# Gaps of 32 bytes between the tiles that the matmuls read, in a four-layer decoder trunk

## Chip, core and metric

The kernel runs on one core of one Trainium2 chip. The metric is the device time of one execution in microseconds (us); the time before is the median of two runs. The profile is one further look at one execution, taken by the hardware profiler.

## The reference

A trunk of two layers on 512 tokens of width 1024, everything in float32. Each layer is a half-step SwiGLU feed-forward block, an attention block and a second half-step SwiGLU block, all with RMS norm ahead of them:

```python
def swiglu(h, w_gate_up, w_down):
    gate, up = jnp.split(h @ w_gate_up, 2, axis=-1)      # 1024 -> 2 x 2816
    return (jax.nn.silu(gate) * up) @ w_down             # 2816 -> 1024

for i in range(DEPTH):                                   # DEPTH = 2
    x = x + 0.5 * swiglu(rms_norm(x, ...), ffn_w_gate_up[i, 0], ffn_w_down[i, 0])
    h = rms_norm(x, norm_gains[i, 1])
    x = x + (stick_breaking_attention(h, ...) if i % 2 == 0 else sliding_window_attention(h, ...))
    x = x + 0.5 * swiglu(rms_norm(x, ...), ffn_w_gate_up[i, 1], ffn_w_down[i, 1])
```

The first attention block weights each key by a sigmoid times the product of what the later keys left over; the second is a windowed softmax with 16 query heads on 2 key heads. Both end with an output projection of 1024 by 1024.

## The kernel before

**Layout.** The residual stream stays on the chip as eight tiles `x0` to `x7` of 128 channels by 512 tokens. Every large product puts weights into the tensor engine as the stationary operand (128 by 128) and streams 512 tokens past them.

**Three passes.** To keep float32 accuracy, each operand is split into a high part and the rest: `norm_tile` (L244) makes `xh` and `xl` of each tile of x, `_part` (L173) makes `whi` and `wlo` of each piece of weights, `swiglu` (L303) makes `hh` and `hl` of each tile of the activations. `terms` (L127) then issues three matmuls for each 128 rows of the contraction: (`whi`, `xh`), (`whi`, `xl`), (`wlo`, `xh`), always in this order. In the profile the group `gu<-xh,whi` is the first of these for the gate and up products, `dn<-hl,whi` the second for the down product. All have the line L75, that of the helper through which the tensor engine's instructions keep the order of the program.

**Stages.** The string "0s12w3" names six stages: feed-forward 0, stick-breaking attention s, feed-forward 1 and 2, window attention w, feed-forward 3. A feed-forward stage (`ffn`, L317) makes 44 products `gu` of 8 x 3 matmuls (22 gates, 22 ups) and then 8 products `dn` of 22 x 3. So the four of them hold 4 x 44 x 24 = 4224 matmuls for gate and up (24 of them in the first stage write to a bank named `gus`) and 4 x 8 x 66 = 2112 for down. `project_out` (L546) makes the 8 x 24 matmuls `op` at the end of an attention stage; `q` and `k` are 8 x 24 each; `tok` are products with 256 columns in which the weights are streamed.

**Weights.** They come as a stream of units of 128 x 1024 or 128 x 896 numbers. A unit is loaded by DMA (`_load`), then copied to `whi` by ScalarE (L181) and subtracted to `wlo` by VectorE (L186, or GpSimd L184). Three units are held at a time, in three buffers of the tag `whi` and three of `wlo`; when the last matmul of a unit has been issued, `release` (L188) opens the next one. Twice, near the end of an attention stage, `advance` (L166) puts one more unit into tiles that the stage no longer needs (`qsw`/`ksw` in stage s, `qw` in stage w).

**Addresses.** A tile is a run of bytes at one address in all partitions. The tiles lie in the order of their allocation, each rounded up to 32 bytes. In the program before, these are the addresses modulo 128 bytes:

| tiles | remainder |
|---|---|
| x, raw, whi, wlo, acc, xh, xl (all of 2048 or 4096 bytes, one behind the other) | 96 |
| everything of a feed-forward stage: hh, hl (behind three small tiles of 32 bytes each) | 64 |
| stage s: qs, ks, kl, v, wt, the attention outputs o..h and o..l, and the spare weights qsw, ksw | 64 |
| stage w: outputs oh, ol | 96 |
| stage w: spare weights qw | 0 |

Slices of a tile that the matmuls read begin at multiples of 512 bytes from its start, so they have their tile's remainder. So a `gu` matmul streams from remainder 96 and its weights lie at 96; a `dn` matmul streams from 64 and its weights lie at 96.

Of the kernel before, what the change touches and what calls it, by code (L numbers as in the profile page):

```python
# [7 lines left out]
F32 = mybir.dt.float32  # L8
F32R = mybir.dt.float32r
# [6 lines left out]
P = 128  # L16
T = 512
TB = T // P
D = 1024
KD = D // P  # L20
# [4 lines left out]
HD = 64  # L25
# [13 lines left out]
NROT = ROT // 2  # L39
# 500000 ** (-arange(0, 16, 2) / 16) in float32  # L40
INV_FREQ = [
# [23 lines left out]
class _Ordered:  # L65
    """an engine whose instructions stay in the order of the program"""

# [19 lines left out]
class _Filler:  # L87
    """tensor-engine work that fills the waits of an attention step: a generator that yields its cost,
    or None when nothing is ready"""

# [17 lines left out]
class _Trunk:  # L108
    def __init__(self, tc, pools, psum, aps):
        self.tc, self.nc = tc, _Engines(tc)  # L110
        self.const, self.work = pools
        self.psum = psum
        self.aps = aps
        self.units = []
        self.raw, self.ready = [], []
        self.taken = self.spent = 0
        self.roped = False
        self.extra = -1

# [1 line left out]
    def mm(self, out, lhs, rhs, start, stop):  # L121
# [5 lines left out]
    def terms(self, out, pairs, first=True, last=True, release=()):  # L127
        """out = sum of w * x over pairs ((w_hi, w_lo), (x_hi, x_lo)): three float32r passes each;
        release: the terms that are the last of a unit of the weight stream, or 1: the last"""
        n = len(pairs)  # L130
        cost = 3 * max(out.shape[-1], 256) / 2400.0
        for i, ((wh, wl), (xh, xl)) in enumerate(pairs):
            self.mm(out, wh, xh, start=(first and i == 0), stop=False)
            self.mm(out, wh, xl, start=False, stop=False)
            self.mm(out, wl, xh, start=False, stop=(last and i == n - 1))
            if i in ((n - 1,) if release == 1 else release):
                self.release(1)
            yield cost
# [7 lines left out]

# [1 line left out]
    def queue(self, ap, pool=False):  # L148
# [11 lines left out]
    def _open(self, n):  # L160
        size = self.units[n][1]
        hi = self.work.tile([P, size], F32R, tag="whi", name=f"whi{n}", bufs=UNITS)
        lo = self.work.tile([P, size], F32R, tag="wlo", name=f"wlo{n}", bufs=UNITS)
        self.ready.append((hi, lo))

    def advance(self, hi, lo):  # L166
        """one more unit of the weight stream ahead, in tiles that the stage has free"""
        n = self.extra = len(self.ready)
        self.ready.append((hi, lo))
        self._part(n)  # L170
        self._load()
# [25 lines left out]
    def weights(self, a):  # L197
        """the next unit of the stream as [row, a, column] high and low parts"""
        hi, lo = self.ready[self.taken]
        self.taken += 1  # L200
        h3, l3 = (t.rearrange("p (a b) -> p a b", a=a) for t in (hi, lo))
        return [(h3[:, i, :], l3[:, i, :]) for i in range(a)]

# [1 line left out]
    def setup(self, which):  # L205
# [36 lines left out]

# [1 line left out]
    def norm_tile(self, k, which):  # L244
        nc, w = self.nc, self.work
        if k == 0:
            self.xh, self.xl = [], []
            self.acc = w.tile([P, T], F32, tag="acc", name="acc", bufs=1)
        g = self.gain[:, which * KD + k : which * KD + k + 1]
        hi = w.tile([P, T], F32R, tag=f"xh{k}", name=f"xh{k}", bufs=1)  # L250
        lo = w.tile([P, T], F32R, tag=f"xl{k}", name=f"xl{k}", bufs=1)
        nc.scalar.activation(hi, self.x[k], AF.Copy, scale=g)
        nc.vector.scalar_tensor_tensor(lo, self.x[k], g, hi, ALU.mult, ALU.subtract)  # L253
        self.xh.append(hi)
        self.xl.append(lo)
        if k == 0:
            nc.scalar.activation(self.acc, self.x[k], AF.Square)
        else:
            sq = w.tile([P, T], F32, tag="rbc", name="sq", bufs=1)
            nc.scalar.activation(sq, self.x[k], AF.Square)  # L260
            (nc.gpsimd if k < POOL_SQUARES else nc.vector).tensor_add(self.acc, self.acc, sq)  # L261
# [39 lines left out]

# [1 line left out]
    def swiglu(self, fp, f, gu):  # L303
        nc = self.nc
        g = fp.tile([P, T], F32, tag="g", name="g", bufs=2)
        u = fp.tile([P, T], F32, tag="u", name="u", bufs=2)
        nc.vector.tensor_mul(g, gu[0], self.rbc)  # L307
        nc.scalar.activation(g, g, AF.Silu)
        nc.vector.tensor_mul(u, gu[1], self.rbc)  # L309
        nc.vector.tensor_mul(u, g, u)  # L310
        hi = fp.tile([P, T], F32R, name=f"hh{f}")
        lo = fp.tile([P, T], F32R, name=f"hl{f}")
        nc.scalar.copy(hi, u)
        nc.vector.tensor_sub(lo, u, hi)
        return hi, lo
# [52 lines left out]

# [1 line left out]
    def stack(self, out, src):  # L370
        """a pair of heads (rows) to one [high | low] or [low | high] column of rows per head"""
        nc = self.nc
        for h in range(2):
            own, other = slice(h * HD, (h + 1) * HD), slice(HD - h * HD, 2 * HD - h * HD)
            nc.scalar.copy(out[own, h, :], src[own, :])
            nc.vector.tensor_sub(out[other, h, :], src[own, :], out[own, h, :])  # L376

    def project_pair(self, p, out, start=False):
        """q^T and k^T of a pair of heads, as exact high and low parts"""
        nc, ap = self.nc, self.ap  # L380
# [30 lines left out]
    def token_columns(self, evacuate, rows=None):  # L411
        """a chunk of 256 columns of an input projection, tokens on partitions"""
        w = self.weights(KD // 2) + self.weights(KD // 2)
        for b in range(TB):
            sl = slice(b * P, (b + 1) * P)
            ps = self.bank("tok")[:, : 4 * HD]
            yield from self.terms(ps, [((h[:, sl], l[:, sl]), w[k]) for k, (h, l) in enumerate(zip(self.xh, self.xl))], release=(KD // 2 - 1, KD - 1) if b == TB - 1 else ())
            if rows and b == 0:
                rows()
            evacuate(b, ps)  # L420

    def project_values(self, out):
        """v of four heads: [token, block, head, high | low]"""
        nc = self.nc
# [11 lines left out]
    def stick_scores(self, i, qk, out):  # L436
        """exclusive products of the kept lengths times beta, for one pair of heads and query block i"""
        nc, ap = self.nc, self.ap
# [25 lines left out]
    def stick_turn(self, i, beta, wt):  # L464
        """weights of query block i to keys on partitions, high and low parts"""
        nc = self.nc
# [47 lines left out]
    def fold(self, o, h, ps):  # L514
        """the products with the high and the low part of v are on rows of their own: add them"""
        t = self.ap.tile([HD, T], F32, tag="tmp", name="fold", bufs=2)
# [10 lines left out]
    def project_early(self, parts, opened):  # L527
        """the first terms of the first output tiles, as far as parts are there"""
        self.settled, self.spare = len(parts), None
# [79 lines left out]

# [1 line left out]
    def rope_tables(self):  # L611
        """cos | cos and -sin | sin of every token's angles: [token, block, 16]"""
        self.roped = True
# [58 lines left out]

# [1 line left out]
    def rope(self, x, heads, engine):  # L674
        """x: [token, block, heads * HD], rotated in place"""
        nc, ap = self.nc, self.ap
# [11 lines left out]
    def head_factor(self, sq, heads, extra):  # L688
        """r * rsqrt(mean of squares of r * raw + eps) * extra, one per token, block, head"""
        nc, ap = self.nc, self.ap  # L690
# [57 lines left out]
    def window_queries(self, c, out):  # L748
        """four heads of q with head dims on partitions (two heads a tile), and their score factors"""
        nc, ap = self.nc, self.ap  # L750
# [20 lines left out]
    def window_scores(self, c, b, qt, y, out):  # L771
        """the softmax of four heads and one block of queries"""
        nc, ap = self.nc, self.ap
# [161 lines left out]

# [1 line left out]
    def store(self, n):  # L937
# [92 lines left out]
```

## Time and profile before

| | us |
|---|---|
| median of 2 runs (lowest, highest) | 1928.41 (1927.27, 1929.55) |
| profiled execution, first to last instruction | 1925.5 |
| TensorE busy | 1895.7 |
| VectorE busy | 970.5 |
| ScalarE busy | 695.1 |
| GpSimd busy | 172.0 |

The profiled execution's own span is 1925.5 us; between it and the median lie 2.9 us, which stand for what is around the span. A matmul's own duration in a row (some 390 ns) is longer than its share of the engine, since matmuls overlap; the pace is read from the distance of their starts.

### The profile page before, as it was taken

The page shows a single profiled execution, that of the slowest core. Times are in us where ns is not written, and L with a number is a line of the kernel's source. Part 1 is how long each engine was busy: PE and PEld are TensorE (multiplying, and loading weights), DVE is VectorE, ACT ScalarE, POOL GpSimd, SP SyncE. Part 2 cuts the span into 40 slices and gives each one's busy share as a digit, 9 for nine tenths or more (in the row PEclk, how much of TensorE's full clock was granted, in tenths as well). Part 3 has the DMA queues.
Part 4 walks back from the last instruction along what each step waited for, and adds up shares of the span by engine and source line. Part 5 has one row for each costly group of instructions (what it writes and reads, how often), then busy time and mean ns, then how long its engine had stood idle before and what let it go on. Part 6 is the DMA issues. An engine that isn't in the chain of part 4 may idle for free.

```text
span 1925.5 us, 22581 instructions
## 1 busy us (share of the span) xinstructions
PE 1895.7 (98%) x8994; PEld 1565.6 (81%) x8994; DVE 970.5 (50%) x1535; ACT 695.1 (36%) x1071; POOL 172.0 (9%) x131
## 2 busy tenths in 40 slices
PE   9999999999999999999999999999998999999999
PEld 7888888877887888888888888888887788888887
DVE  6444433378887644443235444423588664444321
ACT  5333222266675323332223333222357542223211
POOL 1000000233321000000000000000142210000000
PEclk9999999999999999999999999999989999999999
DMA  5233333321112333223333222333221122332331
GB/s 167 98 97 99 96 91 92 103 69 56 49 62 66 99 97 97 92 97 94 97 96 99 92 98 96 93 93 100 81 67 34 29 92 98 99 99 90 103 109 60
DMA packets 49930, 170.52 MB, mean 89 GB/s; under 512 B 5921, under 2 KB 6177, under 8 KB 49825
## 3 DMA queue, kind: packets, MB, share of 16 engines
q1 hardware_dynamic: 49824, 169.07, 27.9%
q8 instruction: 71, 1.16, 0.2%
q14 instruction: 35, 0.28, 0.0%
HBM read 166.96 MB, written 2.10 MB: 88 GB/s over the span
## 4 chain that ended last, share of the span: by engine, by line
PE 84%; DVE 8%; issue 4%; ACT 3%; POOL 1%; DMA 0%; SPq 0%; ACTq 0%; DVEq 0%; POOLq 0%
PE gu L75 49%; PE dn L75 23%; PE op L75 4%; PE tok L75 3%; DVE keep L459 2%; DVE beta L460 1%; PE pv L75 1%; DVE qs L376 1%; DVE wt L482 1%; ACT keep L453 1%; PE sc L75 1%; PE z L75 0%; PE ptr L75 0%; DVE e L793 0%; PE q L75 0%
## 5 line engine op out<-in xcount | busy, mean ns | idle before, releaser
L181 ACT CAST whi<-raw 128x1024 fp32r<-128x1024 f32 (+2 forms) x323 | 330.0, 1022 | 964.8 <-issue 361.6
L75 PE MATMUL gu<-xh,whi 128*128 128x512 f32 x1400 | 545.5, 390 | 1.4 <-ACT whi L181 1.4
L75 PE MATMUL gu<-xh,wlo 128*128 128x512 f32 x1400 | 545.0, 389 | 0.7 <-DVE wlo L186 0.7
L75 PE MATMUL gu<-xl,whi 128*128 128x512 f32 x1400 | 544.8, 389 | 0.5 <-DVE xl L253 0.5
L186 DVE TENSOR_TENSOR wlo<-raw,whi 128x1024 fp32r<-128x1024 f32 (+2 forms) x293 | 349.4, 1193 | 248.2 <-ACT whi L181 245.6
L75 PEld LDWEIGHTS gu<-xh,wlo 128*128 128x128 f32 x1400 | 262.8, 188 | 56.5 <-DVE wlo L186 1.8
L75 PEld LDWEIGHTS gu<-xh,whi 128*128 128x128 f32 x1400 | 262.9, 188 | 56.2 <-ACT whi L181 1.9
L75 PEld LDWEIGHTS gu<-xl,whi 128*128 128x128 f32 x1400 | 262.9, 188 | 55.3 <-DVE xl L253 0.9
L75 PE MATMUL dn<-hh,wlo 128*128 128x512 f32 x704 | 280.9, 399 | 0.0
L75 PE MATMUL dn<-hl,whi 128*128 128x512 f32 x704 | 277.4, 394 | 0.0
L75 PE MATMUL dn<-hh,whi 128*128 128x512 f32 x704 | 276.0, 392 | 0.0
L309 DVE TENSOR_TENSOR u<-gu,rbc 128x512 f32<-128x512 f32 x87 | 60.1, 691 | 274.7 <-PE gu L75 274.7
L75 PEld LDWEIGHTS dn<-hl,whi 128*128 128x128 f32 x704 | 132.1, 188 | 34.3
L75 PEld LDWEIGHTS dn<-hh,whi 128*128 128x128 f32 x704 | 132.2, 188 | 31.5
L75 PEld LDWEIGHTS dn<-hh,wlo 128*128 128x128 f32 x704 | 132.2, 188 | 30.5
L307 DVE TENSOR_TENSOR g<-gu,rbc 128x512 f32<-128x512 f32 x88 | 60.8, 691 | 176.5 <-PE gu L75 176.4
L261 POOL TENSOR_TENSOR acc<-acc,sq 128x512 f32<-128x512 f32 x30 | 46.4, 1547 | 1116.1 <-ACT sq L260 1116.1
L184 POOL TENSOR_TENSOR wlo<-raw,whi 128x512 fp32r<-128x512 f32 x60 | 87.5, 1483 | 164.9 <-ACT whi L181 164.9
L75 PE MATMUL tok<-whi,xh 128*128 128x256 f32 x288 | 86.4, 300 | 0.0
L75 PE MATMUL tok<-whi,xl 128*128 128x256 f32 x288 | 82.4, 286 | 0.1
L75 PE MATMUL tok<-wlo,xh 128*128 128x256 f32 x288 | 82.3, 286 | 0.1
L300 DVE SCALAR_TENSOR_TENSOR x<-dn,x 128x512 f32<-128x512 f32 x32 | 22.1, 691 | 116.5 <-PE dn L75 116.5
(310 smaller groups left out, 1957.4 us busy)
## 6 DMA issues: line engine op xcount, KB each, us to landing
raw<-in_gu_dram SPq DMA_DIRECT2D x173, 512.0 KB, 3.4
raw<-in_dn_dram SPq DMA_DIRECT2D x64, 448.0 KB, 3.3
raw<-in_dn_dram SPq DMA_DIRECT2D x32, 512.0 KB, 3.5
raw<-in_sbqk_dram SPq DMA_DIRECT2D x16, 512.0 KB, 3.4
raw<-in_swin_dram SPq DMA_DIRECT2D x10, 512.0 KB, 3.5
raw<-in_sbv_dram SPq DMA_DIRECT2D x8, 512.0 KB, 3.3
raw<-in_sbo_dram SPq DMA_DIRECT2D x8, 512.0 KB, 3.5
raw<-in_swo_dram SPq DMA_DIRECT2D x8, 512.0 KB, 3.3
```

Source lines behind the costliest of these rows:

```text
L75: return self._tc.keep_in_program_order(method(*args, **kwargs))
L181: nc.scalar.copy(hi[:, s], raw[:, s])
L184: nc.gpsimd.tensor_sub(lo[:, t], raw[:, t], hi[:, t])
L186: nc.vector.tensor_sub(lo[:, s], raw[:, s], hi[:, s])
L261: (nc.gpsimd if k < POOL_SQUARES else nc.vector).tensor_add(self.acc, self.acc, sq)
L300: self.nc.vector.scalar_tensor_tensor(self.x[n], ps, factor, self.x[n], ALU.mult, ALU.add)
L307: nc.vector.tensor_mul(g, gu[0], self.rbc)
L309: nc.vector.tensor_mul(u, gu[1], self.rbc)
L376: nc.vector.tensor_sub(out[other, h, :], src[own, :], out[own, h, :])
L453: nc.scalar.activation(keep[:, :, :n], z[:, :, :n], AF.Sigmoid, scale=-0.125)
L459: nc.vector.tensor_tensor_scan(rev, rev, rev, 1.0, ALU.mult, ALU.bypass)
L460: nc.vector.tensor_mul(beta[:, :, : n - 1], beta[:, :, : n - 1], keep[:, :, 1:n])
```

## The change

`shift` allocates a tile that nothing uses, of 32 bytes per partition (64 in one place), so that what is allocated behind it begins that much later. There is one ahead of each of the three `whi` and `wlo` buffers, ahead of each of the eight `xh` and `xl`, and ahead of each of the 22 `hh` and `hl` of a feed-forward stage. To have gaps between them, the three buffers of `whi` become three tags with one buffer each, taken by the number of the unit modulo 3; the same for `wlo`. No instruction is added or removed.

```diff
+        self.gaps = 0
+        self.normed = False
+
+    def shift(self, pool, size):
+        self.gaps += 1
+        pool.tile([P, size // 4], F32, name=f"gap{self.gaps}")
...
     def _open(self, n):
         size = self.units[n][1]
-        hi = self.work.tile([P, size], F32R, tag="whi", name=f"whi{n}", bufs=UNITS)
-        lo = self.work.tile([P, size], F32R, tag="wlo", name=f"wlo{n}", bufs=UNITS)
+        if n < UNITS:
+            self.shift(self.work, 32)
+        hi = self.work.tile([P, size], F32R, tag=f"whi{n % UNITS}", name=f"whi{n}", bufs=1)
+        if n < UNITS:
+            self.shift(self.work, 32)
+        lo = self.work.tile([P, size], F32R, tag=f"wlo{n % UNITS}", name=f"wlo{n}", bufs=1)
...
     def norm_tile(self, k, which):
...
+        first = not self.normed
+        self.normed = k == KD - 1 or self.normed
+        if first:
+            self.shift(w, 32)
         hi = w.tile([P, T], F32R, tag=f"xh{k}", name=f"xh{k}", bufs=1)
+        if first:
+            self.shift(w, 32)
         lo = w.tile([P, T], F32R, tag=f"xl{k}", name=f"xl{k}", bufs=1)
...
     def swiglu(self, fp, f, gu):
...
+        self.shift(fp, 64 if f == NF // 2 else 32)
         hi = fp.tile([P, T], F32R, name=f"hh{f}")
+        self.shift(fp, 32)
         lo = fp.tile([P, T], F32R, name=f"hl{f}")
```

Added up in the order of allocation, the remainders modulo 128 become:

| tiles | remainder |
|---|---|
| whi, wlo of buffer 0; 1; 2 | 0, 32; 64, 96; 0, 32 |
| xh, xl of even k; of odd k | 64, 96; 0, 32 |
| hh, hl for f up to 10: even f; odd f | 32, 64; 96, 0 |
| hh, hl for f from 11: even f; odd f | 64, 96; 0, 32 |
| stage s, all of its tiles | 0 |
| stage w: oh, ol; qw | 32; 64 |

## Prediction

> **What bounds the kernel now.** First the page: busy shares, granted clock, and the chain that ended last.
>
> ```profile
> span 1925.5 us, 22581 instructions
> PE 1895.7 (98%) x8994; PEld 1565.6 (81%) x8994; DVE 970.5 (50%) x1535; ACT 695.1 (36%) x1071; POOL 172.0 (9%) x131
> PEclk9999999999999999999999999999989999999999
> PE 84%; DVE 8%; issue 4%; ACT 3%; POOL 1%; DMA 0%; SPq 0%; ACTq 0%; DVEq 0%; POOLq 0%
> L75 PE MATMUL gu<-xh,whi 128*128 128x512 f32 x1400 | 545.5, 390 | 1.4 <-ACT whi L181 1.4
> L75 PE MATMUL dn<-hh,whi 128*128 128x512 f32 x704 | 276.0, 392 | 0.0
> ```
>
> TensorE is busy 98% of the span at nearly the full clock, 84% of the chain is its own, and the two groups hardly wait. There are three such groups each, so 4200 matmuls `gu` and 2112 `dn`. Busy time does not say how fast they go. For that I read the chain in order of time, whose long pieces are runs of matmuls that waited for nobody (start, length, count), and the windows of one run each.
>
> ```profile
> 32.88 217.60 PE gu L75 x960
> 250.48 123.21 PE dn L75 x528
> 386.68 11.53 PE tok L75 x96
> ...
> 32.88:250.48 217.60, 217.60 (x962) 180.18 (x961) 102.36 (x124) 66.41 (x84) 0.00 (x0) 1.00 0.30 96
> 250.48:373.69 123.21, 123.21 (x530) 99.11 (x529) 37.02 (x40) 32.93 (x40) 13.05 (x9) 1.00 0.31 92
> ```
>
> In both windows PE is busy all the time and the clock is 1.00, yet 217.60 / 960 is 226.7 ns per matmul and 123.21 / 528 is 233.4 ns, for instructions of the same shape. The tok run has 256 columns and 11.53 / 96 = 120.1 ns. Between 226.7 and 120.1 lie 256 columns, so a column costs 0.416 ns, 512 of them 213.2 ns, and what is left is a fixed cost per matmul: 13.5 ns in gu and tok, 20.2 ns in dn. This fixed cost, some 57 us in gu and 43 us in dn, is all that a change of addresses can touch on the path.
>
> **Is it the address?** The output projections give the comparison: same code, same loop, the moving operand at remainder 64 in stage s and at 96 in stage w, the weights at 96 in both. The rows are the first and the last start of a run on PE's timeline.
>
> ```profile
> 617.16 0.39 PE L75 MATMUL op<-o1h,whi 128*128 128x512 f32 x1
> 621.83 0.39 PE L75 MATMUL op<-o7h,wlo 128*128 128x512 f32 x1
> ...
> 1538.02 0.39 PE L75 MATMUL op<-ol,whi 128*128 128x512 f32 x1
> 1545.95 0.39 PE L75 MATMUL op<-oh,whi 128*128 128x512 f32 x1
> ```
>
> From 617.16 to 621.83 are 20 steps, 233.5 ns each, the pace of dn. From 1538.02 to 1545.95 are 35, 226.6 ns each, the pace of gu. So equal remainders (96 and 96) go with 226.7, and 64 against 96 with 233.4. Why two operands at once: while one matmul streams, the next one's weights are being loaded.
>
> ```profile
> 120.21 0.39 PE L75 MATMUL gu<-xh,wlo 128*128 128x512 f32 x1
> 120.22 0.19 PEld L75 LDWEIGHTS gu<-xh,whi 128*128 128x128 f32 x1
> ```
>
> The load starts 10 ns behind the matmul's start or less and runs beside it. The trace doesn't show where the two meet; that they do is my reading.
>
> There is a third pace, outside the steady pattern. Where a run begins, or the remainders switch, it takes about ten matmuls to settle.
>
> ```profile
> 250.32 0.40 PE L75 MATMUL dn<-hh,whi 128*128 128x512 f32 x1
> 252.44 0.39 PE L75 MATMUL dn<-hh,whi 128*128 128x512 f32 x1
> ...
> 608.82 0.40 PE L75 MATMUL op<-o0h,qsw 128*128 128x512 f32 x1
> 611.36 0.40 PE L75 MATMUL op<-o3h,ksw 128*128 128x512 f32 x1
> ```
>
> The first nine steps of dn behind gu take 2.12 us, 235.6 ns each, and only then does the pattern of 233.4 begin. The eleven steps with the spare weights (64 against 64, equal again) right behind steps of 64 against 96 take 2.54 us, 230.9 ns each: equal remainders without the time to settle are not at 226.7. So the pace depends on the remainders and on what came just before.
>
> **The change, part by part.** *The gaps* remove and add no instruction; all transfers, casts and subtractions stay. What they move are addresses, and the pairs that meet are these (moving operand minus the weights loaded beside it, modulo 128). In gu, 0 or 64, alternating from one k to the next, which is every three matmuls. In dn, 32 or 96 for the first eleven f and 0 or 64 for the other eleven, alternating likewise. Before, it was 0 throughout in gu and 96 throughout in dn. Differences of 32 and 64 occur in no long run of the trace; they are the unknown.
>
> Bounds for a matmul of the changed kernel, by the nearest rows: from below 226.7, the settled pace of equal remainders; from above 235.6, the unsettled pace of unequal ones. A pace below 226.7 can't be excluded, since 13.5 ns of fixed cost are still in it; it is a rival below. Between the ends I take 230.9: it is the measured pace of equal remainders that are not given time to settle, it lies in the middle of 226.7 and 235.6, and a pair that changes every three matmuls leaves no ten to settle.
>
> - gu: 4200 x (230.9 - 226.7) = +17.6 us.
> - dn: 2112 x (230.9 - 233.4) = -5.3 us.
> - op in stage w, 192 matmuls from 226.7 to 230.9: +0.8 us; op in stage s, 192, a third of them at 230.9 already: -0.3 us. q and k outside the first pair stand among attention matmuls and never settle: 0. tok has weights at mixed remainders too; its 864 matmuls at +-2 ns are +-1.7 us, taken as 0.
>
> *The tags.* With buffers chosen by the unit's number, the one unit that goes into spare tiles skips its number, so the next unit finds its buffer held by a unit that is still in use, one unit later than before. This happens twice. In stage w:
>
> ```profile
> 1531.56 1.05 ACT L181 CAST whi<-raw 128x1024 fp32r<-128x1024 f32 x1 [1.75 <-PE op L75]
> 1532.64 1.23 DVE L186 TENSOR_TENSOR wlo<-raw,whi 128x1024 fp32r<-128x1024 f32 x1 [0.16 <-ACT whi L181]
> 1533.66 1.98 ACT L181 CAST whi<-raw 128x1024 fp32r<-128x1024 f32 x2
> 1535.71 0.40 PE L75 MATMUL op<-oh,whi 128*128 128x512 f32 x1
> ```
>
> The cast that starts at 1531.56, when the first output tile is through, would start near 1533.7, when the second is. With the 1.05 of the cast, 0.69 of a residual that VectorE does first and 1.23 of the subtraction, `wlo` is there at about 1536.6; it is wanted by the third matmul behind 1535.71, at about 1536.2. That is 0.4 us late, and behind the waiting cast on ScalarE stand the next unit's cast and a norm tile, for which nobody on the path waits before 1541. In stage s the same shift is covered, since four terms per tile, not two, are left ahead of the unit. I take +0.4, bounds 0 and 1.5. The gaps need no time on SP: the queue of loads is unchanged.
>
> Sum: 17.6 - 5.3 + 0.8 - 0.3 + 0.4 = +13.2 us. Against the profiled execution: 1925.5 + 13.2 = 1938.7 of span; with the 2.9 us by which the median stands above that span, 1941.6, about **1941 us**. On ScalarE and VectorE nothing is near the path in the feed-forward stages (102.36 and 66.41 us busy of 217.60 above), so a slower or faster access there would be covered.
>
> **A rule that speaks against any effect.** The two projections above differ by 6.9 ns per matmul with the operand's place. The Trainium skill says otherwise ("TensorE: Matmul & The Clock Gate", Step-by-step): the engine has two independent read ports, and loading the next weights doesn't take read bandwidth from the running matmul; and "SBUF — State Buffer", Who interferes with whom, says "PE and ACT never wait on anyone." By that rule the sum would be the +0.4 of the tags; the trace disagrees with it.
>
> **Rivals.**
> 1. *Nothing on the path changes* (the difference of paces has another cause, such as the higher address bits, which the gaps leave nearly alone): 1928 to 1929 us. For it: nothing shown. Against it: the two projections. Chance 0.08.
> 2. *Only the remainder modulo 64 counts.* Then gu has a difference of 0 as before and keeps 226.7, the first half of dn keeps 233.4, and the second half, 1056 matmuls, falls to 226.7, less the nine unsettled steps at 230.9 in each of 32 runs: -7.1 + 1.2. With +0.4: 1928.4 - 5.5 = 1923 us. For it: 0 and 96 are the only differences seen, and they are 0 and 32 modulo 64. Against it: nothing. Chance 0.20.
> 3. *The spread takes conflicts away.* If matmul and weight load stand in each other's way because they walk through memory at the same remainder, spreading halves the 13.5 ns and takes dn to the same pace, 220 ns: 4200 x -6.7 - 2112 x 13.4 - 384 x 10 = -60 us, 1868 us; half of it would be 1898. For it: a fixed cost of 13.5 ns is there to be saved. Against it: the equal remainders are the fast case in the trace. Chance 0.18, for 1860 to 1910.
> 4. *Slower: unequal is worse everywhere.* gu takes dn's pace (+6.7 x 4200 = 28.1), dn the unsettled 235.6 (+2.2 x 2112 = 4.6), op of stage w +1.3: with +0.4, 1963 us. It decides if the differences of 32 and 64 cost at least as much as 96 does. For it: the only unequal pair seen is the slow one. Against it: half of gu and a quarter of dn still have difference 0. Chance 0.12, for 1955 to 1975.
>
> A limit for rival 3, from the Trainium skill alone ("TensorE: Matmul & The Clock Gate", Back-to-back issue gap): N / 2.4 + 2.5 ns, 215.8 for 512 columns. By it gu and dn would give 4200 x 10.9 + 2112 x 17.6 = 83 us, so the estimate for the very best is 1846. No run here shows such a pace.
>
> **How the numbers follow.** The forecast, unsettled paces for both, has the remaining 0.42 and covers 1930 to 1955. A measurement of this kernel can tell about 2% from no change, here below 1890 or above 1967. Rival 3 puts 0.15 below 1890 and the slow rival 0.05 above 1967; one in a hundred on each side is left for what I haven't seen. So faster 0.16, within 2% 0.78, slower 0.06. The range leaves out the faster half of rival 3 and the slow end of rival 4: 1880 to 1965; the forecast's own is 1930 to 1955.
>
> **What would show it.** In the chain over time, the gu run of 960 at 217.60 should become 221 to 222 us and the dn run of 528 at 123.21 about 122. Rival 2 shows gu unchanged and dn fast in its second eleven f only; rival 3 shows gu below 215; rival 4 gu above 223 and dn above 123. The steady 226.7 in gu should be gone: steps differ within each k. The tags show as casts that end later near 1533, with a gap on PE under 1.5 us. I am wrong if differences of 32 or 64 have a settled pace far from those seen, or if the fixed cost comes from the change of operand from one matmul to the next, and not from the pair that meets.

## The result, and the profile after

The changed kernel takes 1943.20 us (median of 2 runs, 1942.95 to 1943.46) against 1928.41 us: a ratio of 1.0074, 95% interval 1.0045 to 1.0103. It is slower by 0.7%, less than the 2% by which a measurement of this kernel can tell from no change; but the interval leaves out 1, and the trace shows where the time went. The profiled execution took 1942.95 us with a span of 1940.8 us, 15.3 us more than the span before.

The page of the changed kernel, the lines that answer to those shown of before, and two groups of gate and up matmuls:

```profile
span 1940.8 us, 22580 instructions
...
PE 1908.3 (98%) x8994; PEld 1563.4 (81%) x8994; DVE 971.1 (50%) x1535; ACT 693.6 (36%) x1071; POOL 172.6 (9%) x131
...
PEclk9999999999999999999999999999989999999999
...
PE 85%; DVE 8%; issue 4%; ACT 2%; POOL 1%; DMA 0%; SPq 0%; DVEq 0%; ACTq 0%; POOLq 0%
...
L75 PE MATMUL gu<-xl,whi 128*128 128x512 f32 x1400 | 551.8, 394 | 0.6 <-DVE xl L270 0.6
L75 PE MATMUL gu<-xh,whi 128*128 128x512 f32 x1400 | 550.9, 393 | 0.8 <-ACT whi L192 0.8
```

The other engines' busy times are the same within 2 us, TensorE's is 12.6 us longer for as many matmuls, and the two groups wait less than 1 us each in all. The granted clock is 1.00 in the long runs of gu and dn, as before. So the time went into the matmuls themselves. How much goes where is read from the chain in order of time, as before (start, length, what and how many):

```profile
33.13 221.70 PE gu L75 x960
254.83 122.45 PE dn L75 x528
...
390.36 11.33 PE tok L75 x96
...
611.11 32.05 PE op L75 x138
...
655.64 232.76 PE gu L75 x1008
...
1541.04 28.45 PE op L75 x120
```

The row of before for op in stage s is wanted too, and that of stage w:

```profile
606.84 32.19 PE op L75 x138
...
1529.86 27.81 PE op L75 x120
```

221.70 / 960 is 230.9 ns per gu matmul (226.7 before), 122.45 / 528 is 231.9 ns per dn matmul (233.4 before). For all 4200 and 2112 that is +17.9 and -3.0 us; op takes 0.1 us less in stage s and 0.6 us more in stage w. The sum, +15.4, is the 15.3 of the span to a tenth. That it is so close is partly chance: the stretch from tok to op in stage s, which the sum leaves out, is 0.6 us longer too (220.8 us, 220.2 before).

Inside gu the steady pace is gone. Distances from start to start in the trace, in ns, from 100.18 us on:

```
229 230 230 232 230 230 232 236 228 228 234 235 229 229 230 232
```

### The profile page after: what moved, and what is told of

Same layout as the page of the kernel before. It is cut to its first block, busy times and chain, and to the rows that moved or that the text cites. A ratio compares the mean times of both kernels' runs of the same rounds, so it can differ in the third digit from the quotient of the medians.

```text
span 1940.8 us, 22580 instructions
## 1 busy us (share of the span) xinstructions
PE 1908.3 (98%) x8994; PEld 1563.4 (81%) x8994; DVE 971.1 (50%) x1535; ACT 693.6 (36%) x1071; POOL 172.6 (9%) x131
## 4 chain that ended last, share of the span: by engine, by line
PE 85%; DVE 8%; issue 4%; ACT 2%; POOL 1%; DMA 0%; SPq 0%; DVEq 0%; ACTq 0%; POOLq 0%
PE gu L75 49%; PE dn L75 23%; PE op L75 4%; PE tok L75 3%; DVE keep L478 2%; PE pv L75 1%; DVE beta L479 1%; DVE qs L395 1%; PE q L75 1%; DVE wt L501 1%; PE sc L75 1%; PE z L75 1%; ACT keep L472 1%; PE ptr L75 0%; DVE e L812 0%
## 5 line engine op out<-in xcount | busy, mean ns | idle before, releaser
L75 PE MATMUL gu<-xl,whi 128*128 128x512 f32 x1400 | 551.8, 394 | 0.6 <-DVE xl L270 0.6
L75 PE MATMUL dn<-hh,wlo 128*128 128x512 f32 x704 | 276.8, 393 | 0.0
```

Of the source, the lines that this page charges most:

```text
L75: return self._tc.keep_in_program_order(method(*args, **kwargs))
```

## The experiments

The prediction's theory was that a matmul's fixed cost depends on the difference of two addresses modulo 128 bytes, those of the moving operand and of the weights that are loaded beside it. Each expectation below says which theories it sets against each other. `gap(pool, size)` allocates a tile that nothing uses, as the change's `shift` does. A kernel that was run once is read by its trace, against the span of 1925.5 us and the paces of before.

### Constant differences

Four kernels move all tiles xh and xl by one amount, and all hidden tiles (hh, hl) and the o tiles of stage s by one amount, so that differences stay constant. `d0_aligned` has the 32-byte gaps at the head of the feed-forward and of the stage s pool alone; the others have a gap of 32, 64 or 96 bytes ahead of x as well.

```diff
@@ setup @@
+        self.gap(self.work, 32)          # d32_all; 64 in d64_all, 96 in d96_all; not in d0_aligned
@@ feed-forward @@
         with tc.tile_pool(name="ffn", bufs=1) as fp:
+            self.gap(fp, 32)
@@ stage s @@
         with tc.tile_pool(name="stick", bufs=1) as self.ap:
+            self.gap(self.ap, 32)
```

> The kernel before with one gap of 32 bytes at the start of the feed-forward and stick-breaking pools, so that hh, hl and the attention outputs lie at remainder 96 like x and the weights: difference 0 in every large product. Theory 1 (the settled pace follows the difference between the moving operand and the weights loaded beside it): dn falls from 233.4 to 226.7 ns, the chain's run of 528 from 123.2 to 119.7 us, the time by 2112 x 6.7 + 192 x 6 = 15 us to 1913, ratio 0.992. Rival (streams that walk at the same remainder stand in each other's way): dn doesn't fall, 1928 or more.

> Weights at remainder 96, x and hh, hl and the attention outputs at 0: difference 32 in every large product, constant through each run. Theory 1: gu and dn get one common settled pace, between 226.7 and 236 ns; by the mean of the changed kernel about 231. Theory 2 (what costs is the change of remainder from one matmul to the next): constant remainders settle at 226.7 in both, 1913 us.

> Weights at 96, x and hh, hl and the attention outputs at 32: difference 64 throughout. Theory 1: one common settled pace for gu and dn; if only the remainder modulo 64 counts it is 226.7 (1913 us), otherwise between 226.7 and 236. Theory 2: 226.7 in both. Rival (streams at the same remainder stand in each other's way): this is the fastest of the four, below 226.7.

> Weights at 96, x and hh, hl and the attention outputs at 64: difference 96 throughout. Theory 1: gu takes the pace that dn had before, 233.4 ns, the chain's run of 960 goes from 217.6 to 224.0 us, the time to 1928.4 + 28 + 1 = 1957. Theory 2 and any theory in which dn was slow for a reason of its own: gu stays at 226.7, 1928.

`d0_aligned` took 1928.18 us (10 runs) against 1927.46: ratio 1.0004 (0.9994 to 1.0013). The gain in dn isn't there. Chain over time, `d0_aligned`:

```profile
33.56 217.60 PE gu L75 x960
251.16 123.19 PE dn L75 x528
```

The dn matmuls stay at 233.3 ns, though hidden tiles and weights now share their remainder modulo 128. Their addresses explain it: the weights lie at 96 and the hidden tiles at 224 modulo 256. The same trace has steps in which both operands lie at 224 modulo 256, those of op with the spare weights. The first eleven lie between these two rows:

```profile
608.96 0.39 PE L75 MATMUL op<-o0h,qsw 128*128 128x512 f32 x1
611.46 0.40 PE L75 MATMUL op<-o3h,ksw 128*128 128x512 f32 x1
```

They take 2.50 us, 227.3 ns each. The next eleven such steps, from o4h to o7h, take 2.54 us, 230.9 ns each, as the first ones of before did. The distances from start to start, in ns, show why the means differ:

```
o0h to o3h   231 227 226 227 227 226 227 227 226 227 227
o4h to o7h   235 233 236 224 231 236 228 233 230 227 227
```

Both end at the fast pace; the second takes ten steps to reach it. So agreement modulo 128 is not enough, and modulo 256 may be; the second group of experiments tries it. The other three, in the chain over time of `d32_all`, `d64_all` and `d96_all`:

```profile
35.03 224.00 PE gu L75 x960
...
259.03 123.70 PE dn L75 x528
```

```profile
34.06 219.73 PE gu L75 x960
253.79 123.19 PE dn L75 x528
...
390.00 10.89 PE tok L75 x96
```

```profile
33.77 224.00 PE gu L75 x960
257.77 123.19 PE dn L75 x528
```

By differences modulo 256: gu at 32 and at 96 has 224.00 / 960 = 233.3 ns, dn's old pace, and at 64 it has 228.9 ns; dn has 234.3 ns at 160 (`d32_all`), and 233.3 at 192 (`d64_all`) and at 224 (`d96_all`). So gu and dn of `d64_all`, both 64 apart modulo 128, differ by 4.4 ns: again the smaller modulus is not enough. The spans were 1956.9, 1935.2 and 1953.6 us. `d32_all` differs from `d0_aligned` by the gap ahead of x alone, with not one instruction changed, and gu goes from 226.7 to 233.3 ns: addresses set the pace.

Are they TensorE's own reads, or does other engines' traffic at the moved tiles slow it? In the gu run of `d96_all`, from 45 to 240 us, every distance over three steps is 700 ns to the nanosecond, 833 times, while VectorE starts 159 instructions and ScalarE 105. A disturbance by their accesses would hardly come in step with the matmuls.

### The period, the pair, the load and the tags

```diff
# align256: as d0_aligned, with 160 in place of 32: all these tiles at 96 modulo 256
+            self.gap(fp, 160)
+            self.gap(self.ap, 160)

# pair_hi_lo: gaps so that whi, xh, hh lie at 96 and wlo, xl, hl at 128 modulo 256

# half_loads: in terms(), the second and third matmul of a term use 64 columns of the weights,
# but for the last term of a product or unit
+            half = i < n - 1 and wh.shape[-1] == P and out.shape[-1] == T
+            c = P // 2 if half else P
-            self.mm(out, wh, xl, start=False, stop=False)
-            self.mm(out, wl, xh, start=False, stop=(last and i == n - 1))
+            self.mm(out[:c], wh[:, :c], xl, start=False, stop=False)
+            self.mm(out[:c], wl[:, :c], xh, start=False, stop=(last and i == n - 1))

# tags_only: _open() with three tags of one buffer, and no gaps
+        hi = self.work.tile([P, size], F32R, tag=f"whi{n % UNITS}", name=f"whi{n}", bufs=1)
+        lo = self.work.tile([P, size], F32R, tag=f"wlo{n % UNITS}", name=f"wlo{n}", bufs=1)
```

> The kernel before with a gap of 160 bytes at the start of the feed-forward and stick-breaking pools, so that hh, hl and the attention outputs lie at 96 modulo 256, as x and the weights do. Theory 1b (the settled pace follows the difference to the weights loaded beside, modulo 256; only 0 gives 226.7 ns): dn falls from 233.4 to 226.7, its run of 528 from 123.2 to 119.7 us, the time by 2112 x 6.7 + some 150 x 6 = 15 us to 1912, ratio 0.992. Theory 3 (the 226.7 of gu has nothing to do with dn's addresses): dn stays at 233.3 as it did with 32 bytes, ratio 1.000.

> High parts (whi, xh, hh) at 96 modulo 256, low parts (wlo, xl, hl) at 128. Then every matmul of gu and dn has difference 0 to the weights that are loaded beside it, although the moving operand's remainder changes by 32 with every matmul and the weights in use lie 0, 32 and -32 away. If the load beside it is what counts: gu and dn both settle at 226.7 ns (runs of 960 and 528 at 217.6 and 119.7 us). If the weights in use count, or the step from one moving operand to the next: 231 to 234 ns in both (222 to 224 us and 122 to 123.5).

> The kernel before, but the second and third pass of every 128 rows except the last in a unit or product use only the first 64 of 128 columns of the weights, so two of three weight loads are half as long; the low-part corrections of the other 64 outputs are left out. Number and length of the streams are the same. If the fixed cost comes from the load that runs beside the stream, it falls by about a third: dn from 20.2 to 13 to 15 ns (226 to 228 per matmul), gu from 13.5 to 9 to 13. If it comes from the change from one stream to the next, both keep their pace, 226.7 and 233.4.

> The kernel before with the three tags of one buffer for whi and wlo and no gap. Predicted +0.4 us, between 0 and 1.5: 1928 to 1929, ratio 1.000; the cast that starts at 1531.6 before starts near 1533.7, and the stream of the next output tile waits under 1.5 us. Rival: the tags are what costs the 15 us, 1943.

`align256` took 1911.11 us (4 runs, 1909.50 to 1911.61) against 1927.77: ratio 0.9912 (0.9897 to 0.9927). It beats both kernels. Chain over time:

```profile
33.46 217.60 PE gu L75 x960
251.06 119.68 PE dn L75 x528
...
383.68 11.53 PE tok L75 x96
...
601.82 31.36 PE op L75 x138
```

dn has come down to 119.68 / 528 = 226.7 ns, gu's pace, which for 2112 matmuls is 14.1 us; op in stage s gives 0.8 us. That is 14.9 of the 16.7 us between the medians. So agreement modulo 256 bytes is enough: modulo 512 the hidden tiles lie 256 bytes off the weights here, and are at the fast pace all the same.

`pair_hi_lo`, one run, span 1946.4 us. Each matmul's moving operand has the remainder of the weights loaded beside it, and still:

```profile
34.49 222.93 PE gu L76 x960
257.42 122.61 PE dn L76 x528
```

Both stages have 232.2 ns. So equality with the weights loaded beside is not enough, which is against the pair as the prediction had it.

`half_loads`, one run, span 1937.4 us:

```profile
34.53 220.14 PE gu L75 x960
254.67 122.75 PE dn L75 x528
```

Two loads of three are half as wide in 1204 of the 1400 terms of gu and in 608 of the 704 of dn. Such a load takes 134 ns where a wide one takes 188, not half of it. Still gu is slower, 229.3 ns, and dn is at 232.5 ns, 0.9 below before; neither of the two outcomes expected came. The fixed cost does not follow the amount of weights loaded. Why gu lost its pace isn't settled: the edit also shortens what a matmul writes, and wide and narrow matmuls alternate.

`tags_only` took 1928.00 us (10 runs) against 1927.77: ratio 1.0004 (0.9994 to 1.0014). No effect of the tags alone is seen; the interval leaves room for 2.7 us, not for 15.

### Which operands have to agree

```diff
# alt_k: blocks 4 to 7 of x and of a weight tile 32 bytes further on, the blocks of gu taken in turn;
# casts and subtractions of weights are split at the gap, and some constants are smaller
+                        pairs = [pairs[i] for i in (0, 4, 1, 5, 2, 6, 3, 7)]

# wlo32: as align256, but wlo at 128 modulo 256, and a gap of 224 behind it that keeps x at 96
+        if n == 0:
+            self.gap(self.work, 32)
         lo = self.work.tile([P, size], F32R, tag="wlo", name=f"wlo{n}", bufs=UNITS)

# abs64: as align256, all of it moved to 192 modulo 256
+        self.gap(self.work, 96)
         for n in range(UNITS):
             self._load(2)

# hs_only: the change's gaps of hh and hl, and no others
+        self.gap(fp, 64 if f == NF // 2 else 32)
         hi = fp.tile([P, T], F32R, name=f"hh{f}")
+        self.gap(fp, 32)
         lo = fp.tile([P, T], F32R, name=f"hl{f}")
```

> In the gate and up matmuls the eight blocks of x and of the weights are taken in the order 0, 4, 1, 5, 2, 6, 3, 7, and blocks 4 to 7 of both lie 32 bytes further on: the two operands of one matmul always share a remainder modulo 256 bytes, but from one term of three matmuls to the next the remainder goes from 96 to 128 and back. The tiles of the down projection stay unaligned. Theory U (it is the weights in use that count against the moving operand): every difference is 0, the run of 960 gu takes 217.6 us, 226.7 ns each. Theory L (the weights loaded beside count): every third matmul has 32 bytes between the two, the run takes 219 to 222 us. Theory S (what disturbs is a change of remainder from one matmul's operands to the next one's): changes at every third matmul, 219 to 223 us, near the 222.9 us of the kernel whose high and low parts lie apart.

> All tiles at 96 modulo 256 bytes, as in the aligned kernel, but the low parts of the weights 32 bytes further on. Moving operands never change their remainder. Theory S for the moving operand alone: nothing disturbs, the run of 960 gu takes 217.6 us and 528 dn 119.7 us. Theories U and L alike (a difference of 32 bytes at one matmul of three, the third or the second): by the settled paces (2 x 226.7 + 233.3) / 3 = 228.9 ns, 219.7 us and 120.9 us, and up to the 232.2 ns of the kernel with high and low parts apart, 222.9 us and 122.6 us. The whole span then 1920 to 1935 us.

> The aligned kernel moved as a whole by 96 bytes: weights, x and hidden tiles all lie at 192 modulo 256 bytes, where they lay at 96. If only differences count: 226.7 ns everywhere, gu 217.6 us, dn 119.7 us, span 1907.6 us as measured there. If the place itself counts, another pace, up to the 233.3 ns of before's dn, whose moving tiles lay at 192: span up to 1949 us.

> Of the change only the gaps of the hidden tiles hh and hl. If the two stages add up: gu at 226.7 ns (217.6 us for 960) as before, dn at the 231.9 ns of the changed kernel (122.4 us for 528), span 1925.5 - 3.1 = 1922.4 us. If the gaps of x and of the weights are needed for the gain in dn: dn between 122.4 and 123.7 us, span 1922 to 1927 us.

Each was run once; spans 1953.1, 1954.1, 1912.0 and 1923.2 us. Chain over time of `alt_k`, then of `wlo32`, `abs64` and `hs_only`:

```profile
34.24 222.93 PE gu L75 x960
```

```profile
34.56 224.00 PE gu L75 x960
...
258.56 123.20 PE dn L75 x528
```

```profile
34.45 217.60 PE gu L75 x960
252.05 119.68 PE dn L75 x528
...
384.67 11.52 PE tok L75 x96
...
605.86 31.36 PE op L75 x138
```

```profile
34.03 217.60 PE gu L75 x960
251.63 122.37 PE dn L75 x528
```

- `alt_k`: the weights in use always share the moving operand's remainder, and gu has 232.2 ns. Theory U falls. The load beside differs at one matmul of three and the run is 0.9 us above what theory L allowed; with `pair_hi_lo` theory L has fallen as well.
- `wlo32`: the moving operands never change their remainder, and gu and dn have 233.3 ns. Theory S for the moving operand alone falls. So does any price per matmul by its own difference: two of three matmuls have none, and the mean is not 228.9, nor within the 232.2 that I gave as the end. It is the full pace of a constant difference of 32.
- `abs64`: 226.7 ns in both stages, as in `align256`. At these two places, 96 and 192, not the place counts, only that the operands agree. Its span is 4.4 us longer than that of `align256`, none of it in the long runs: 1.0 us lies ahead of the first gu run, and 3.1 us between the tok and the op run of stage s, 221.2 us apart here, 218.1 in `align256` and 220.2 before. With one run this is not told from the attention stage's own spread.
- `hs_only`: dn has 231.8 ns, as in the changed kernel, while gu keeps 226.7. The stages add up: the gaps of the hidden tiles are a small gain, the gaps of x and of the weights are the loss.

What the twelve runs show together: 226.7 ns was measured where moving operands, high weights and low weights of neighbouring matmuls all lie at one remainder modulo 256 bytes, and in no other long run. With some of them elsewhere, or all changing together, the pace is between 228.9 and 234.3 ns. Agreement alone does not give it either: in `half_loads` all operands of gu agree, and it has 229.3 ns. Which part of the hardware makes it so stays open: the trace shows no wait inside a matmul, and no single pair of addresses accounts for the paces.

## Why the prediction was right, and where not

- **What bounds the kernel** was right: TensorE's matmuls carried the whole change, and the fixed cost was where it came from. `align256` took dn's fixed cost from 20.2 to 13.5 ns, gu's figure. The fall of 6.7 ns is measured; the split into columns and fixed cost is not firm. It rests on tok's 120.1 ns, and with the 228.9 and 113.4 ns of `d64_all` the same subtraction leaves less than nothing for the fixed cost.
- **"Is it the address?"** Right, with a wrong period. The moving operands of the two projections, at 64 and 96 modulo 128, lay at 192 and 96 modulo 256, the weights at 96; both readings fit the rows, and I took the smaller modulus without a row that told them apart. `d0_aligned` (233.3 ns) against `align256` (226.7 ns) does.
- **The pair that meets**, the moving operand and the weights loaded beside it, was the wrong step. `pair_hi_lo` keeps that pair equal throughout and has 232.2 ns. The prediction's last sentence named this way of being wrong, a change of operand from one matmul to the next; that fits `alt_k` and `pair_hi_lo`, but a constant difference (`d32_all`) costs as much, so it is not the whole either.
- **The term of gu**, 4200 x 4.2 = +17.6 us, measured +17.9. The value, 230.9 ns, was met to a tenth; its reason was not. It was read as equal remainders that aren't given time to settle. But `pair_hi_lo`, whose remainders change at every matmul, settles into a pattern of its own at 232.2 ns. And 230.9 is no pace of equal remainders: it is the mean of eleven steps on their way to 226.7, as the two rows of `d0_aligned` show, and the steps from o0h to o3h of the changed kernel itself, equal again, have 226.6 from the first one on. That the eleven steps of before and the mixture of the changed kernel have the same mean is a coincidence as far as the runs show; that the truth had to lie between 226.7 and 235.6 was the sound part.
- **The term of dn**, -5.3 us, measured -3.0: 231.9 ns where 230.9 was taken. Same sign, mis-sized by 2.3 us.
- **op**: +0.8 and -0.3 forecast, +0.6 and -0.1 measured in the runs of 120 and 138. The 192 of stage w were not all at 226.7 before: 24 of them have the weights qw, at another remainder. **tok**: taken as 0; the run of 96 went from 11.53 to 11.33 us, 2.1 ns per matmul, just past the bound given, and what it saves is not seen in the sum, since the attention stages around it vary by as much.
- **The tags**, +0.4 us: the step failed, harmlessly. The first casts of stage w do not start later. In `tags_only` and in the changed kernel, the first cast on ScalarE after the start of the op run:

```profile
1528.56 1.05 ACT L186 CAST whi<-raw 128x1024 fp32r<-128x1024 f32 x1 [1.75 <-PE op L75]
```

```profile
1542.73 1.05 ACT L192 CAST whi<-raw 128x1024 fp32r<-128x1024 f32 x1 [1.75 <-PE op L75]
```

The op run begins at 1541.04 in the changed kernel, so the cast comes 1.69 us behind it; before it was 1531.56 - 1529.86 = 1.70 us. The second comes 3.28 us behind the start in both, 3.80 us before. The rows do not carry the number of a unit, so why none had to wait for its buffer stays open. The whole op run of `tags_only` is as long as that of before, 27.82 us:

```profile
1526.86 27.82 PE op L75 x120
```

- **Sum**: +13.2 forecast, +15.3 measured; 1941 us forecast, 1943.2 measured. Most of the difference is dn's term. Small slips changed nothing: 1941.6 rounds to 1942; the 2.9 us added for what is around the span are too many, since in the profiled execution of the changed kernel time and span are 1942.95 - 1940.8 = 2.15 us apart; of the busy times beside gu, 102.36 us is VectorE's and 66.41 us ScalarE's.
- **Rival 1** (nothing changes) is excluded by the ratio's interval. The higher address bits that it named did count, one of them: the bit of 128 bytes. **Rival 2** (remainder modulo 64) falls with gu, and with `d64_all`, where a difference of 64 has 228.9 ns. **Rival 3** (the spread takes conflicts away) has the sign wrong: no long run of 512 columns went below 226.7 ns, and agreement is the fast case. The limit that was set beside it is not one in the section that it names: N / 2.4 + 2.5 ns is there, in the Trainium skill, the gap of an isolated matmul, and a shorter sustained spacing stands beside it. (Its sum gives 1845 us, not 1846.) **Rival 4** (unequal is worse everywhere) is wrong in its numbers for this change, gu 221.7 us and not above 223, dn 122.4 and not above 123; but its mechanism is what a constant difference of 32 or 96 does.
- **The rule of two independent read ports** (the Trainium skill, "TensorE: Matmul & The Clock Gate", Step-by-step), by which nothing but the tags would have shown: modulo 256 `wlo32` and `align256` differ by the place of the low weights alone, and 233.3 against 226.7 ns disagrees with it for these operands.

## What to carry to other kernels

Where a stage is nothing but matmuls back to back, divide the length of a run by its count and compare the stages: two paces for one shape of instruction are a lead, here worth 0.9% of the whole. For matmuls of 512 columns like these, give all operands that stream together, moving and stationary, high and low, the same address modulo 256 bytes, with one gap ahead of a pool, and measure the pace again; spreading the addresses is the loss here. A remainder read off two rows has to be tried at more than one modulus before a change is built on it.

## What the runs showed of the hardware that I had not expected

The uneven steps are not noise; they repeat. Distances from start to start in gu from 80 us on, in ns:

```
align256    227 226 227 227 226 227 227 226 227 227 226 227
d64_all     226 229 231 226 229 232 226 229 232 226 229 231
wlo32       239 229 232 239 229 232 239 229 232 239 229 232
pair_hi_lo  228 235 226 234 229 234 235 234 235 230 236 230
alt_k       241 224 235 231 226 235 230 236 231 228 235 235
```

The pattern has 3 steps in `d64_all` and `wlo32` and 12 in `pair_hi_lo` and `alt_k`, and from the runs of 960 its length is 686.7, 700.0 and 2786.6 ns. With the 226.7 of `align256` these are 103, 105, 418 and 34 times 6.667 ns, each to within 0.1 ns. The length need not be a multiple of the three matmuls of a term: dn in `d32_all` repeats after 7 steps and 1640 ns, 246 times 6.667. It looks as if a matmul's operands are served in slots of that length; the runs don't show by what.

The same alignment does not help every width. In `d64_all` the 256-column matmuls of tok, 10.89 / 96 = 113.4 ns, are faster than the 120.1 ns that they have where all tiles agree: agreement was best for 512 columns and not for 256.
